# A hybrid decoder layer on one core: q and k stacks and most blocks of normalised x transposed on TensorE and copied out of PSUM by ScalarE, in place of DMA transposes

## Chip, cores and metric

The kernel runs on one core of one Trainium2 chip. The metric is the device time of one execution in microseconds (us), from the first to the last instruction and the little that lies around them. Lower is better.

## What is computed

One decoder layer on x of 2048 rows by 1024 columns, in float32: a normalisation, one wide input projection, three causal token mixers side by side, gates, and an output projection. Cut to what matters:

```python
h = rms_norm(x, norm_g)
proj = einsum('bsd,de->bse', h, w_in)          # fq fk fv fg ff px pg sq sk sv sg
fq, fk = rms_norm(heads(fq, 8), q_norm_g), rms_norm(heads(fk, 8), k_norm_g)
log_f = log_sigmoid(ff + b_f)
# A) forgetting attention, 8 heads of 64:
#    softmax(q.k/8 + c[t] - c[s], s <= t) @ v,  c = cumsum(log_f)
fox = forgetting_attention(fq, fk, fv, log_f) * silu(fg)
# B) causal means over 2, 4, 8, 16 rows, a small linear map per group
pool = multiscale_pool(px, w_pool, pool_scale) * silu(pg)
# C) stick-breaking attention, 4 heads of 64, z = q.k/8, s < t:
#    A[t,s] = sigmoid(z_ts) * prod_{s<j<t} (1 - sigmoid(z_tj))
sb = stick_breaking_attention(sq, sk, sv) * silu(sg)
out = x + concat([fox, pool, sb]) @ w_out
```

## The kernel before

Rows are worked on in 16 blocks of 128, last block first (block index i, row block j = 15 - i, so the keys that block i needs are those of blocks already done). Five phases follow each other and overlap: "a" (heads 0 to 3 of the forgetting attention), "b" (heads 4 to 7), "s" (stick-breaking, 4 heads), "p" (pooling, strewn between the blocks of "s") and "o" (output projection). Every number is kept as a pair of float16 values, a high part and the rest ("hi" and "lo"), so a product takes two or three matmuls.

For each block of phase "a" the rows of x are normalised, split into hi and lo (tile `ppx`, 128 x 2048 float16), and transposed into `xTx` (16 squares of 128) by one DMA transpose on SP's queue (`transpose_rows`, L375). The transposed block is parked in DRAM and read back in phases b, s and p. The projection (`project`, L319) then gives q and k in one PSUM tile and v and the gate in another. For q and k the function `stacks` (L455) makes a tile `st` (`sta`, `stb`, `sts` by phase) that holds k as hi and lo and q as hi and lo for four heads; one DMA transpose (L464) turns it into `qT`. Five steps of the projection later (`SCD`) `place` copies the k half into the key store `K` (L467) and swaps the two halves of q (L469, twice), all on VectorE. Scores (`scores`, L404) multiply `qT` with `K` into a PSUM tile with the tag `sp`. There are two buffers of that tag, each of two banks of PSUM, and each score tile holds one until VectorE (phases a and b, L736) or ScalarE (phase s, L875) has read it. The weights that come out are split into hi and lo (`split_t`: hi on ScalarE or VectorE L430 and L432, lo on GpSimd L433, tile `pp`), transposed by DMA (L435, tile `tt`) and multiplied with V (L446, L447, L903 to L905) three heads later. The tiles `pp` come from `PB` buffers.

A planner with its own estimate of every duration puts the instructions of each engine in order ahead of time; each engine then runs its list strictly in that order and waits at the head of it. Tables such as `LEADS` and `PAT` say how many projection steps are mixed in between the heads. All DMA transposes are issued from SP's queue. The clock of TensorE is granted by the chip, at 2.4 or 1.2 GHz.

Of the kernel before, what the change touches and what calls it, by code (L numbers as in the profile page):

```python
# [10 lines left out]
F16 = mybir.dt.float16  # L11
BF16 = mybir.dt.bfloat16
AF = mybir.ActivationFunctionType
ALU = mybir.AluOpType
# [4 lines left out]
P = 128  # L19
KT = 8  # L20
D = 1024
HD = 64
NH = 4
# [13 lines left out]
GR4 = 0  # L37
GR2 = 1
QSB = 2
SWE = 'vv'  # L40
KCE = 'v'
SCD = 5
M5 = 2
FE = 's'
OMS = 'g'
# [17 lines left out]
LEAD = 10  # L63
DEPTH = 3
TB = 4
PB = 5
FHIA = 'sv'
FHIB = 'ssv'
FLO = 'gg'
# [56 lines left out]
def hybrid(ctx: ExitStack, tc, xN, w_in, w_pT, w_out, ng, b_f, qg, kg, w_pool, p_scale, bands, out):  # L126
    nc = tc.nc
    v, s, g, t, sy = nc.vector, nc.scalar, nc.gpsimd, nc.tensor, nc.sync
# [4 lines left out]
    const = ctx.enter_context(tc.tile_pool(name="const", bufs=1))  # L133
# [3 lines left out]
    at = ctx.enter_context(tc.tile_pool(name="at", bufs=2))  # L137
    sm = ctx.enter_context(tc.tile_pool(name="sm", bufs=3))
    pj = ctx.enter_context(tc.tile_pool(name="pj", bufs=PJ, space=PSUM))
    ps = ctx.enter_context(tc.tile_pool(name="ps", bufs=2, space=PSUM))  # L140
# [5 lines left out]
    def pick(pattern, k):  # L146
        return {"v": v, "g": g, "s": s}[pattern[k % len(pattern)]]
# [31 lines left out]
    ident = const.tile([P, P], F32, name="ident")  # L179
# [4 lines left out]
    g.affine_select(tri, ones, [[-1, P]], ALU.is_ge, 0.0, base=0, channel_multiplier=1)  # L184
    id16 = const.tile([P, P], BF16, name="id16")
    g.tensor_copy(id16, ident)
    zero = at.tile([P, P], BF16, name="zero", tag="oa")
    g.memset(zero, 0.0)
    cmask = const.tile([P, P], BF16, name="cmask")
# [37 lines left out]
    class Weights:  # L227
# [12 lines left out]
        def measure(self, kt):  # L240
            for a, n in enumerate(self.widths):
                wr = self.raw(kt, a, "wm")
                junk = at.tile([P, n], BF16, name=f"jk{self.name}_{kt}_{a}", tag="pp", bufs=PB)
                acc = self.fa[:, a * KT + kt:a * KT + kt + 1]
# [53 lines left out]
        def weigh(self, kt, eng):  # L298
            held = self.held[:, kt]
            junk = at.tile([P, self.widths[0]], BF16, name=f"jh_{kt}", tag="L", bufs=LB) if eng is s else at.tile([P, self.widths[0]], BF16, name=f"jh_{kt}", tag="pp", bufs=PB)  # L300
            acc = self.fa[:, kt:kt + 1]
# [37 lines left out]
    def pairs16(hi, lo, src, scale, eng=v):  # L339

        s.activation(hi, src, AF.Copy, scale=scale)
        eng.scalar_tensor_tensor(lo, src, scale, hi, ALU.mult, ALU.subtract)  # L342
# [28 lines left out]
    def transpose_rows(src, scale, tag, park=None):  # L371
        pp = at.tile([P, 2 * D], F16, name=f"pp{tag}", tag="pp", bufs=PB)
        pairs16(pp[:, 0:D], pp[:, D:2 * D], src, scale[:, 0:1], pick(XLO, park or 0))
        x = xp.tile([P, 2, KT, P], F16, name=f"xT{tag}", tag="xT", bufs=XB)
        sy.dma_start_transpose(x.rearrange("p a k t -> p (a k) t"), pp)  # L375
        if park is not None:
            keep_x(park, x)
        return x

# [70 lines left out]
    def heads(ap):  # L450
        return ap.rearrange("p (h d) -> p h d", h=NH)
# [2 lines left out]

    def stacks(tag, j, qsrc, ksrc, sc, Kc):  # L455

        st = at.tile([P, 2, NH, P], F16, name=f"st{tag}", tag="qs", bufs=QSB)
        pairs16(st[:, 0, :, 0:HD], st[:, 0, :, HD:P], heads(ksrc), sc)
        pairs16(st[:, 1, :, 0:HD], st[:, 1, :, HD:P], heads(qsrc), sc)
        qT = at.tile([P, 2 * NH, P], F16, name=f"qT{tag}", tag="qT", bufs=QTB)  # L460
        if j % 4 == 3:
            Kc[j // 4] = big.tile([P, NH, 512], F16, name=f"K{tag}", tag="K", bufs=KB)
        o_ = (j % 4) * P
        sy.dma_start_transpose(qT, st.rearrange("p a h d -> p (a h d)"))  # L464

        def place():
            pick(KCE, 0).tensor_copy(Kc[j // 4][:, :, o_:o_ + P], qT[:, 0:NH])  # L467
            for k in range(2):
                pick(SWE, k).tensor_copy(qT[k * HD:k * HD + HD, 0:NH], qT[HD - k * HD:P - k * HD, NH:2 * NH])  # L469
            placed.add(tag)  # L470

        later(SCD, place)
        return qT
# [839 lines left out]
```

## Time and profile before

| | before |
|---|---|
| runs | 1418.04 us median of 3 (1412.04 to 1418.87) |
| the profiled execution | 1417.73 us |
| its span, first to last instruction | 1415.7 us |
| mean granted TensorE clock | 0.937 of 2.4 GHz |
| busy: TensorE, VectorE, ScalarE, GpSimd | 85%, 70%, 50%, 45% |
| mean busy share of the DMA engines, phases a and b | 97% |

The profiled execution lies 0.3 us under the median and 2.0 us over its own span. Phase a takes the span from about 46 to 462 us, b to 821 us, s (with p) to 1280 us, and the end of o the rest. Busy shares are means over these stages.

### The profile page before, as it was taken

What the parts mean: (1) busy time and instruction counts of PE and PEld (TensorE: products, weight loads), DVE (VectorE), ACT (ScalarE), POOL (GpSimd) and SP (SyncE); (2) the same over time, 40 slices, a digit from 0 to 9 for tenths busy, and PEclk for the clock granted to TensorE, in tenths of its full rate; (3) what the DMA queues carried; (4) which work ended last, traced back from release to release, by engine and by line L of the source; (5) the groups of instructions that cost most, each with busy time, mean ns of one, the idle gap of its engine ahead of it and who ended that gap; (6) DMA issues with size and microseconds to landing.
All of it is one profiled execution on the core that took longest, in us unless ns stands there. A gap on an engine that the chain in (4) does not pass through costs nothing.

```text
span 1415.7 us, 24981 instructions
## 1 busy us (share of the span) xinstructions
PE 1209.6 (85%) x9068; PEld 642.2 (45%) x9068; DVE 997.1 (70%) x2093; ACT 702.0 (50%) x1356; POOL 634.1 (45%) x615
## 2 busy tenths in 40 slices
PE   7788879787887889897987888978988997779998
PEld 3344445444444445454544544444544553444443
DVE  5777889889998567786888655556574669865731
ACT  6555546555554446664667644545455564432210
POOL 0133345445455234553656654555455464623300
PEclk9889899999998989999999999999999999989999
DMA  6689999998999999996999998687886888999853
GB/s 215 176 169 203 214 188 221 200 196 182 210 210 209 210 227 207 202 177 135 184 217 191 227 207 186 146 158 161 173 175 142 172 196 226 225 277 287 225 160 89
DMA packets 617068, 275.25 MB, mean 194 GB/s; under 512 B 552561, under 2 KB 590833, under 8 KB 616945
## 3 DMA queue, kind: packets, MB, share of 16 engines
q1 hardware_dynamic: 605600, 239.93, 80.4%
q10 hardware_dynamic: 10832, 33.67, 7.9%
q8 instruction: 71, 1.16, 0.4%
q14 instruction: 53, 0.43, 0.1%
q0 software_dynamic: 512, 0.07, 0.0%
HBM read 102.60 MB, written 34.67 MB: 97 GB/s over the span
## 4 chain that ended last, share of the span: by engine, by line
PE 18%; DVE 11%; issue 9%; DMA 8%; POOL 8%; ACT 5%; SPq 1%; POOLq 0%; ACTq 0%; DVEq 0%
PE pr L319 11%; DVE rrs L883 5%; POOL pps L433 5%; DMA qTs<-sts 2%; DMA qTb<-stb 2%; PE pqks L319 2%; DVE Lb L736 2%; DMA xTm<-ppm 1%; ACT pps L430 1%; ACT Lb L746 1%; POOL rrs L877 1%; PE sps L404 1%; DMA ttb<-ppb 1%; PE pp L319 1%; POOL ppb L433 1%
## 5 line engine op out<-in xcount | busy, mean ns | idle before, releaser
L433 POOL TENSOR_TENSOR ppb<-Lb,ppb 128x1024 f16<-128x1024 f32 (+7 forms) x96 | 151.6, 1593 | 150.3 <-ACT ppb L430 68.9
L433 POOL TENSOR_TENSOR ppa<-La,ppa 128x1024 f16<-128x1024 f32 (+7 forms) x96 | 152.7, 1604 | 141.9 <-DVE ppa L432 53.4
L433 POOL TENSOR_TENSOR pps<-rrs,pps 128x640 f16<-128x640 f32 (+7 forms) x96 | 171.3, 1790 | 75.2 <-ACT pps L430 74.8
L319 PE MATMUL pr<-wo,xTm 128*128 128x512 f16 x768 | 172.2, 386 | 8.1 <-DMA xTm<-ppm 5.3
L883 DVE TENSOR_TENSOR_SCAN rrs<-rrs 128x640 f32<-128x640 f32 (+7 forms) x64 | 109.5, 1714 | 68.3 <-POOL rrs L877 43.8
L430 ACT CAST pps<-rrs 128x640 f16<-128x640 f32 (+7 forms) x96 | 76.1, 796 | 142.0 <-DVE rrs L883 127.3
L746 ACT ACTIVATE Lb<-Lb,nmb 128x640 f32<-128x640 f32 (+7 forms) x96 | 85.6, 892 | 80.3 <-DVE nmb L740 75.4
L746 ACT ACTIVATE La<-La,nma 128x640 f32<-128x640 f32 (+7 forms) x96 | 85.5, 891 | 77.0 <-DVE nma L740 53.5
L319 PEld LDWEIGHTS <-xTm 128*128 128x128 f16 x768 | 75.8, 99 | 100.9 <-issue 8.8
L319 PEld LDWEIGHTS <-xTb 128*128 128x128 f16 x768 | 77.0, 103 | 92.6 <-issue 16.7
L404 PE MATMUL spa<-Ka,qTa 128*128 128x512 f16 (+3 forms) x320 | 83.7, 371 | 36.8 <-DVE mma L736 35.2
L319 PEld LDWEIGHTS <-xTs 128*128 128x128 f16 x768 | 74.4, 99 | 86.9 <-issue 3.3
L319 PEld LDWEIGHTS <-xTx 128*128 128x128 f16 x720 | 72.6, 105 | 89.3 <-issue 25.5
L319 PE MATMUL pqkb<-wb,xTb 128*128 128x512 f16 x384 | 101.7, 408 | 0.3 <-ACT wb L277 0.3
L404 PE MATMUL spb<-Kb,qTb 128*128 128x512 f16 (+3 forms) x320 | 79.7, 361 | 23.4 <-DVE mmb L736 20.7
L319 PE MATMUL pp<-auxp,xTp 128*128 128x512 f16 x384 | 96.9, 404 | 0.0
L319 PE MATMUL pqka<-wa,xTx 128*128 128x512 f16 x336 | 95.3, 434 | 1.3 <-DVE cr L562 1.3
L319 PE MATMUL pvgb<-wb,xTb 128*128 128x512 f16 x384 | 96.1, 390 | 0.0
L875 ACT ACTIVATE rrs<-sps,nc 128x640 f32<-128x640 f32 (+7 forms) x96 | 80.5, 863 | 30.3 <-PE sps L404 28.8
L319 PE MATMUL pqks<-ws,xTs 128*128 128x512 f16 x384 | 92.1, 385 | 0.7 <-DVE vo L342 0.4
L404 PE MATMUL sps<-Ks,qTs 128*128 128x512 f16 (+3 forms) x320 | 73.2, 361 | 21.2 <-DVE qTs L469 16.6
L319 PE MATMUL pvgs<-ws,xTs 128*128 128x512 f16 x384 | 90.9, 379 | 0.0
(307 smaller groups left out, 2804.4 us busy)
## 6 DMA issues: line engine op xcount, KB each, us to landing
xn<-in_xN_dram SPq DMA_DIRECT2D x16, 512.0 KB, 5.5
xTd<-xTx ACTq DMA_DIRECT2D x16, 512.0 KB, 4.3
xTb<-xTd ACTq DMA_DIRECT2D x16, 512.0 KB, 4.6
xTs<-xTd ACTq DMA_DIRECT2D x16, 512.0 KB, 4.3
xTp<-xTd ACTq DMA_DIRECT2D x16, 512.0 KB, 4.3
go<-gat SPq DMA_DIRECT2D x16, 512.0 KB, 7.6
mt<-mix SPq DMA_DIRECT2D x16, 512.0 KB, 5.6
xr<-in_xN_dram SPq DMA_DIRECT2D x16, 512.0 KB, 4.4
```

The costliest lines, as they stand in the source:

```text
L319: t.matmul(psum, x[:, xa, kt, :], wt[:, wa, c0:c0 + n], start=(kt == 0 and i == 0), stop=(kt == KT - 1 and i == 2))
L404: t.matmul(sp[:, b - c0 + off:e - c0 + off], qT[:, a * NH + h, :], Kc[b // 512][:, h, b % 512:b % 512 + e - b], start=(a == 0), stop=(a == ...
L430: s.copy(hi, p32)
L433: lo_eng.tensor_tensor(lo, p32, hi, ALU.subtract)
L736: v.tensor_tensor_reduce(lt, sp, negc[:, h, c0:c1_], c1[:, 0:1], 4 * NEG if a == 0 else mm[:, a - 1:a], ALU.add, ALU.max, mm[:, a:a + 1])
L746: s.activation(ls[a], ls[a], AF.Exp, bias=nm[:, 0:1], accum_out=la[:, a, h:h + 1])
L875: s.activation(gg, sp, AF.Sigmoid, scale=self.nc2[:, 0:1])
L877: g.affine_select(gg[:, 0:P], gg[:, 0:P], [[1, P]], ALU.is_gt, 1.0, base=0, channel_multiplier=-1)
L883: v.tensor_tensor_scan(gg, gg, gg, init, ALU.mult, ALU.bypass)
```

## The change

In `transpose_rows` the blocks that get parked are transposed by 16 TensorE transposes into a new PSUM tile `pt`, which takes one of the two `sp` buffers, and ScalarE copies it out in two pieces. In the program that is so for 14 of the 16 blocks of x; blocks 13 and 14, which the opening makes, and the 16 blocks of the output phase stay with the DMA. In `stacks` the tile `st` gets a third section: k as hi and lo, q's hi twice, q's lo twice. ScalarE writes hi of q over 512 instead of 256 columns, and VectorE makes lo of q in two passes instead of one. `place` makes 12 TensorE transposes into a `pt` tile, and two ScalarE copies bring out the keys and `qT`. The swap is no longer needed. `SCD` falls from 5 to 2 and `PB` from 5 to 4.

```diff
--- before.py
+++ after.py
@@ -37,9 +37,7 @@
 GR4 = 0
 GR2 = 1
 QSB = 2
-SWE = 'vv'
-KCE = 'v'
-SCD = 5
+SCD = 2
 M5 = 2
 FE = 's'
 OMS = 'g'
@@ -63,7 +61,7 @@
 LEAD = 10
 DEPTH = 3
 TB = 4
-PB = 5
+PB = 4
 FHIA = 'sv'
 FHIB = 'ssv'
 FLO = 'gg'
@@ -184,6 +182,8 @@
     g.affine_select(tri, ones, [[-1, P]], ALU.is_ge, 0.0, base=0, channel_multiplier=1)
     id16 = const.tile([P, P], BF16, name="id16")
     g.tensor_copy(id16, ident)
+    idh = const.tile([P, P], F16, name="idh")
+    g.tensor_copy(idh, ident)
     zero = at.tile([P, P], BF16, name="zero", tag="oa")
     g.memset(zero, 0.0)
     cmask = const.tile([P, P], BF16, name="cmask")
@@ -372,8 +372,14 @@
         pp = at.tile([P, 2 * D], F16, name=f"pp{tag}", tag="pp", bufs=PB)
         pairs16(pp[:, 0:D], pp[:, D:2 * D], src, scale[:, 0:1], pick(XLO, park or 0))
         x = xp.tile([P, 2, KT, P], F16, name=f"xT{tag}", tag="xT", bufs=XB)
-        sy.dma_start_transpose(x.rearrange("p a k t -> p (a k) t"), pp)
-        if park is not None:
+        if park is None:
+            sy.dma_start_transpose(x.rearrange("p a k t -> p (a k) t"), pp)
+        else:
+            pt = ps.tile([P, 2048], F16, name=f"pt{tag}", tag="sp")
+            for b in range(2 * KT):
+                t.transpose(pt[:, b * P:(b + 1) * P], pp[:, b * P:(b + 1) * P], idh)
+            for a in range(2):
+                s.copy(x[:, a], pt[:, a * D:(a + 1) * D].rearrange("p (k t) -> p k t", k=KT))
             keep_x(park, x)
         return x
 
@@ -454,19 +460,28 @@
 
     def stacks(tag, j, qsrc, ksrc, sc, Kc):
 
-        st = at.tile([P, 2, NH, P], F16, name=f"st{tag}", tag="qs", bufs=QSB)
+
+        st = at.tile([P, 3, NH, P], F16, name=f"st{tag}", tag="qs", bufs=QSB)
         pairs16(st[:, 0, :, 0:HD], st[:, 0, :, HD:P], heads(ksrc), sc)
-        pairs16(st[:, 1, :, 0:HD], st[:, 1, :, HD:P], heads(qsrc), sc)
+        hi, lo = (st[:, a].rearrange("p h (r d) -> p h r d", r=2) for a in (1, 2))
+        s.activation(hi, heads(qsrc).unsqueeze(2).broadcast_to([P, NH, 2, HD]), AF.Copy, scale=sc)
+        for r in range(2):
+            v.scalar_tensor_tensor(lo[:, :, r], heads(qsrc), sc, hi[:, :, r], ALU.mult, ALU.subtract)
         qT = at.tile([P, 2 * NH, P], F16, name=f"qT{tag}", tag="qT", bufs=QTB)
         if j % 4 == 3:
             Kc[j // 4] = big.tile([P, NH, 512], F16, name=f"K{tag}", tag="K", bufs=KB)
         o_ = (j % 4) * P
-        sy.dma_start_transpose(qT, st.rearrange("p a h d -> p (a h d)"))
 
         def place():
-            pick(KCE, 0).tensor_copy(Kc[j // 4][:, :, o_:o_ + P], qT[:, 0:NH])
-            for k in range(2):
-                pick(SWE, k).tensor_copy(qT[k * HD:k * HD + HD, 0:NH], qT[HD - k * HD:P - k * HD, NH:2 * NH])
+            pt = ps.tile([P, 2048], F16, name=f"pt{tag}", tag="sp")
+            for h in range(NH):
+                t.transpose(pt[:, 1024 + h * P:1024 + (h + 1) * P], st[:, 0, h, :], idh)
+            for a in range(2):
+                for h in range(NH):
+                    b = (a * NH + h) * P
+                    t.transpose(pt[:, b:b + P], st[:, 1 + a, h, :], idh)
+            s.copy(Kc[j // 4][:, :, o_:o_ + P], pt[:, 1024:1536].rearrange("p (h b) -> p h b", h=NH))
+            s.copy(qT, pt[:, 0:1024].rearrange("p (h b) -> p h b", h=2 * NH))
             placed.add(tag)
 
         later(SCD, place)
```

Counted over the program, 800 transposes come to TensorE, 124 copies to ScalarE and 48 passes to VectorE; 144 copies leave VectorE and 62 DMA transposes leave SP's queue. The planner then orders much anew. Three places, all at block 8 of the stick-breaking phase, show what the prediction speaks of. Names carry the block, the head and a buffer number.

TensorE before, from the last scores of block 7 (`sps_7_3`) through the projection of v and gate (`pvgs_8`) to the first scores of block 8 (`sps_8_0`):

```order
L404 MATMUL sps_7_3_0_11587<-Ks_0_9518,qTs_7_11141 128x512
...
L319 MATMUL pvgs_8_11549<-ws_6_9114,xTs7_11302 128x512
...
L319 MATMUL pvgs_8_11549<-ws_7_9119,xTs7_11302 128x512
L404 LDWEIGHTS qTs_8_11546
L404 MATMUL sps_8_0_0_11671<-Ks_8_11547,qTs_8_11546 128x128
...
L404 MATMUL sps_8_0_0_11671<-Ks_4_10419,qTs_8_11546 128x512
```

TensorE now, at the same place; `pts_8` is the new PSUM tile and `sts_8` the stack:

```order
L478 MATMUL pts_8_12290<-idh_157,sts_8_12275 128x128
...
L482 MATMUL pts_8_12290<-idh_157,sts_8_12275 128x128
...
L410 MATMUL sps_7_3_0_12336<-Ks_0_10157,qTs_7_11864 128x512
...
L319 MATMUL pvgs_8_12283<-ws_7_9745,xTs7_12036 128x512
L482 LDWEIGHTS sts_8_12275
...
L410 LDWEIGHTS qTs_8_12281
L410 MATMUL sps_8_0_0_12417<-Ks_8_12282,qTs_8_12281 128x128
```

Eight of the twelve transposes stand ahead of the scores of block 7, and the last four directly ahead of the first scores of block 8.

VectorE before, in the same stretch (the scans L883 are listed as SCALAR_TENSOR_TENSOR; `sts` is the lo part of the stack):

```order
L342 SCALAR_TENSOR_TENSOR sts_8_11541<-pqks_8_11438,sts_8_11541 128x4x64 x2
L883 SCALAR_TENSOR_TENSOR rrs_7_2_0_11525<-rrs_7_2_0_11525 128x1024
L910 SCALAR_TENSOR_TENSOR oms_6_11583<-os_6_11367,io_9126,oms_6_11583 128x256
L467 COPY Ks_8_11547<-qTs_8_11546 128x4x128
L469 COPY qTs_8_11546<-qTs_8_11546 64x512 x2
L883 SCALAR_TENSOR_TENSOR rrs_7_3_0_11592<-rrs_7_3_0_11592 128x1024
```

VectorE now:

```order
L342 SCALAR_TENSOR_TENSOR sts_8_12275<-pqks_8_12172,sts_8_12275 128x4x64
L898 SCALAR_TENSOR_TENSOR rrs_7_2_0_12259<-rrs_7_2_0_12259 128x1024
L469 SCALAR_TENSOR_TENSOR sts_8_12275<-pqks_8_12172,sts_8_12275 128x4x64 x2
L925 SCALAR_TENSOR_TENSOR oms_6_12332<-os_6_12101,io_9752,oms_6_12332 128x256
L898 SCALAR_TENSOR_TENSOR rrs_7_3_0_12341<-rrs_7_3_0_12341 128x1024
```

The three copies that wait for the DMA are gone from between the scans, and the two passes for q's lo stand behind one scan more.

ScalarE now, in the same stretch (`pps` is the hi part of the split, L890 the sigmoid of the scores); before, there were no COPY rows here:

```order
L467 ACTIVATE sts_8_12275<-pqks_8_12172 128x512
L436 CAST pps_7_2_0_12266<-rrs_7_2_0_12259 128x1024
L890 ACTIVATE rrs_7_3_0_12341<-sps_7_3_0_12336,nc2_9750 128x1024
L391 DMA xTp13_12040<-xTd13_126 128x2048
L483 COPY Ks_8_12282<-pts_8_12290 128x4x128
L484 COPY qTs_8_12281<-pts_8_12290 128x1024
L436 CAST pps_7_3_0_12348<-rrs_7_3_0_12341 128x1024
```

The two copies that the first scores of block 8 need stand on ScalarE behind a cast that waits for a scan and a sigmoid that waits for the scores of block 7.

## Rows read from the trace of the kernel before

**Rows 1.** The page: span, busy time and share of two engines.

```profile
span 1415.7 us, 24981 instructions
PE 1209.6 (85%) x9068; PEld 642.2 (45%) x9068; DVE 997.1 (70%) x2093; ACT 702.0 (50%) x1356; POOL 634.1 (45%) x615
```

**Rows 2.** Four stretches: length, busy us (instructions) by engine, granted clock, DMA share, GB/s.

```profile
46.00:462.00 416.00, 342.84 (x2594) 185.83 (x2593) 350.29 (x943) 222.88 (x511) 188.81 (x150) 0.91 0.97 201
462.00:821.00 359.00, 309.03 (x2313) 169.25 (x2312) 260.22 (x610) 207.14 (x435) 180.60 (x154) 0.95 0.97 197
821.00:1280.00 459.00, 393.10 (x3418) 211.08 (x3415) 292.58 (x347) 222.96 (x333) 236.53 (x286) 0.94 0.85 189
1280.00:1416.00 136.00, 129.32 (x608) 58.19 (x603) 64.77 (x98) 18.68 (x17) 25.32 (x9) 0.99 0.64 187
```

**Rows 3.** DMA issues: engine, number, median us from issue to landing.

```profile
xTx<-ppx SPq DMA_TRANSPOSE x16, 4.5
...
qTs<-sts SPq DMA_TRANSPOSE x16, 3.7
```

**Rows 4.** Waits of VectorE: us in total, times, longest.

```profile
DVE Ks L467 <- DMA qTs<-sts: 35.5, 12, 5.4
...
DVE Kb L467 <- DMA qTb<-stb: 23.5, 12, 5.9
...
DVE Ka L467 <- DMA qTa<-sta: 13.9, 8, 3.0
```

**Rows 5.** Waits of TensorE: us in total, times, longest.

```profile
PE spa L404 <- DVE mma L736: 35.2, 20, 4.9
PE spb L404 <- DVE mmb L736: 20.7, 13, 4.1
PE ob L446 <- DMA ttb<-ppb: 20.6, 16, 3.9
...
PE sps L404 <- DVE qTs L469: 16.6, 5, 7.1
PE pf L328 <- DMA xTx<-ppx: 11.0, 7, 2.8
PE oa L446 <- DMA tta<-ppa: 10.7, 6, 3.2
PE os L903 <- DMA tts<-pps: 8.6, 8, 3.1
```

**Rows 6.** The chain that ended last, shares of the span by engine and line.

```profile
PE 18%; DVE 11%; issue 9%; DMA 8%; POOL 8%; ACT 5%; SPq 1%; POOLq 0%; ACTq 0%; DVEq 0%
PE pr L319 11%; DVE rrs L883 5%; POOL pps L433 5%; DMA qTs<-sts 2%; DMA qTb<-stb 2%; PE pqks L319 2%; DVE Lb L736 2%; DMA xTm<-ppm 1%; ACT pps L430 1%; ACT Lb L746 1%; POOL rrs L877 1%; PE sps L404 1%; DMA ttb<-ppb 1%; PE pp L319 1%; POOL ppb L433 1%
```

**Rows 7.** VectorE in order of time: start, length, idle before it, releaser.

```profile
934.96 0.29 DVE L467 COPY Ks<-qTs 128x512 f16<-128x512 f16 x1 [4.46 <-DMA qTs<-sts]
```

**Rows 8.** TensorE in order of time, same stretch.

```profile
935.93 2.10 PE L404 MATMUL sps<-Ks,qTs 128*128 128x128 f16 x6 [7.12 <-DVE qTs L469]
```

**Rows 9.** The window after that wait, columns as in group 2, with TensorE loads second.

```profile
936.00:943.00 7.00, 7.00 (x58) 3.81 (x59) 6.05 (x5) 4.72 (x8) 4.05 (x4) 0.81 0.36 72
```

**Rows 10.** TensorE in order of time: nine pairs of V matmuls, then scores.

```profile
601.58 0.22 PE L446 MATMUL ob<-Vb,ttb 128*128 128x128 f16 x1
...
602.34 0.38 PE L404 MATMUL spb<-Kb,qTb 128*128 128x256 f16 x2
```

**Rows 11.** ScalarE groups of one shape: busy us, mean ns, idle before.

```profile
L430 ACT CAST pps<-rrs 128x1024 f16<-128x1024 f32 x28 | 29.2, 1044 | 55.0 <-DVE rrs L883 43.7 <-DMA tts<-pps 6.3 <-DVE mx L1038 5.0
...
L430 ACT CAST pps<-rrs 128x512 f16<-128x512 f32 x20 | 12.4, 618 | 15.8 <-DVE rrs L883 14.4 <-DMA tts<-pps 1.4
```

**Rows 12.** All work of L469, then of L467, on VectorE: us (instructions).

```profile
0.00:1416.00 1416.00, 51.07 (x96) 0.94 0.89 194
...
0.00:1416.00 1416.00, 26.30 (x48) 0.94 0.89 194
```

**Rows 13.** All lo passes into `stb` on VectorE: us (instructions).

```profile
0.00:1416.00 1416.00, 22.85 (x32) 0.94 0.89 194
```

## The prediction, made before the change was run

> **What bounds the kernel now.** I read the page first. TensorE is busy 1209.6 of 1415.7 us, the longest of all engines, so it stands idle for 206 us [rows 1]. The windows by stage show that this holds throughout: TensorE is busy 82% in phase a, 86% in b and 86% in s, at a granted clock of 0.91, 0.95 and 0.94. The DMA engines are nearly full beside it, 0.97 of their time in a and b and 0.85 in s, and VectorE is busy 84% of phase a [rows 2]. So two resources are close to full in a and b, and the change moves work from the fuller one, the DMA, to the other. The list of waits then says what the 206 us are made of. TensorE waits 55.9 us for VectorE to empty a score buffer (35.2 in a, 20.7 in b), 39.9 us for transposed weights to land (20.6, 10.7 and 8.6), 16.6 us for the swapped q of phase s, and 11.0 us for a transposed x [rows 5]. Last I read the chain that ended last. TensorE is 18% of the span there. The landings of transposed stacks of s and b are 2% each, some 57 us together [rows 6]. VectorE's own list shows why they lie there: its copies into the key store stand at the head of its queue for 35.5 + 23.5 + 13.9 = 72.9 us until a stack has landed [rows 4].
>
> One place shows the mechanism. At block 8 of phase s VectorE stands idle for 4.46 us, until the stack has landed at 934.96 us [rows 7], copies and swaps, and TensorE, which has no other work ahead of the scores, has by then waited 7.12 us [rows 8].
>
> **The change, part by part.** Time here is TensorE's busy time, its idle time, and 2 us around the span, so each part is priced by what it does to one of these. I start from the profiled execution, 1417.7 us, which lies 0.3 us under the median of the runs shown; that difference is left out.
>
> Transposes on TensorE. There are 48 x 12 + 14 x 16 = 800. Each streams 128 columns and has a load of 128 columns of its own, like the first matmul of a pair with V. Nine such pairs, each of 128 and 64 columns, take 602.34 - 601.58 = 0.76 us from start to start, 84 ns for 192 columns, so 56 ns for 128 [rows 10]. That makes 45 us at 2.4 GHz, and 48 us at the mean granted clock of 0.937. How much of it moves the end is bounded by two rows. TensorE's 18% stand in a chain that reaches back over about 60% of the span (the sum of its shares), which is 30% [rows 6]: then 14 us. Its busy share is 85% [rows 1]: then 41 us. Neither is nearer, since the list is in order but the waits behind a transpose can shrink by what is put ahead of them. I take the middle, **+28 us**.
>
> The same row speaks on a rule of the Trainium skill, page "TensorE: Matmul & The Clock Gate", section "Part 4: PE-mode transpose". It says that a 128 x 128 transpose was measured at about 275 ns within a kernel. By that figure 800 would cost an estimated 220 us, and the sum below would be some 1610 us; that speaks strongly against the change. The rows of this case give the same kind of duration for one matmul, 0.22 us, while the next starts 56 ns later, so I take the spacing for the price, and the sum does not use the page's figure.
>
> Copies on ScalarE. Nothing in the trace copies float16 out of PSUM there; the nearest rows are the casts of 1024 columns at 1.04 us and 512 columns at 0.62 us [rows 11]. So 48 x (1.04 + 0.62) + 28 x 1.04 = 109 us, and the wider q passes add at most 48 x 0.2 = 10 us. The engine goes from 702 to about 820 us, 58% of the span, and is at most 58% busy in any stage of the trace before, so most of it lies beside other work. On the chain ScalarE is 5 of 60 parts, 8% [rows 6], which gives **+10 us**. The lower bound is 0. The upper is half of it, 60 us, if the copies were queued behind scans as often as ScalarE is busy. Queued behind them are sigmoids and exponentials, so the scores' buffers and GpSimd's split would come later.
>
> VectorE. The copies and swaps that go were 51.1 + 26.3 = 77.4 us [rows 12], and the 72.9 us of standing at the head go too. The 48 extra passes come to 48 x 0.71 = 34 us by those into `stb`, 22.85 us for 32 [rows 13]. Net some 116 us of 1070 us, 11%, leave a queue that TensorE waits 55.9 us for. By that share **-6 us**; bounds 0 and, if every such wait came from the stacks, -56.
>
> The path of q. Before, a stack took a landing of 3.7 us [rows 3] and 77.4/48 = 1.6 us of copies, 5.3 us. Now, once the stack is there, four or twelve transposes (0.2 to 0.7 us) and two copies (1.7 us) come to 1.9 to 2.4 us, so some two thirds of the wait goes. The smaller price for that wait is TensorE's own, 16.6 us [rows 5], two thirds of which is 11. The larger is the chain's 57 us [rows 6], two thirds of which is 38. I take the middle, **-25 us**: not all of VectorE's late scans delay a matmul. In most blocks the planner puts much matmul work between the transposes and the first scores; at the place shown it puts none, so there ScalarE's copies are the next thing to be late.
>
> The path of x. 11.0 us of waits [rows 5] came with a landing of 4.5 us [rows 3]. Now 16 transposes and two copies are 0.9 + 2.1 = 3.0 us. A third goes, **-4 us**; bounds 0 and -11.
>
> DMA load. By the shapes, phase a transposed 35.7 MB of weights, 8.4 of x and 4.2 of stacks; 7.3 and 4.2 MB leave, 24%. In b and s 4.2 of 39.9 MB leave, 10.5%. If waits for weights fall in proportion, 0.24 x 10.7 + 0.105 x (20.6 + 8.6) is **-6 us**. They could fall by all 39.9 if the 0.97 were the whole cause, or not at all: each weight tile waits three heads in the pipeline anyway, and `PB` falls from 5 to 4, which takes a buffer from the same tiles.
>
> The score buffers. The two `sp` buffers now also serve 62 transposes, 46 of them in a and b beside 192 score tiles. A score tile waits 55.9/192 = 0.29 us on average there [rows 5]; at that price 46 more users cost **+13 us**. Bounds: 0, where the planner finds a free buffer, and 46 x 1.66 = 76 us, if the tile behind each one always waits for both copies. Most tiles did not wait at all (33 of 192 did), so the low value is nearer.
>
> SP's 62 issues and the planner's other moves I cost at nothing, since SP's queue waits for data, not the other way, and a transfer that starts sooner is covered by the three heads between split and use; without that cover a start delayed by one issue would cost about a landing, 4 us, each time. The sum: 28 + 10 - 6 - 25 - 4 - 6 + 13 = +10, so 1417.7 + 10 = **1428 us**.
>
> **The rivals.**
>
> The chain is right (chance 0.30). VectorE's stand for a landing was what delayed everything, and the nearly full DMA lets go too: the q path gives 38 us, x 4, VectorE 6, and the weights half of their 39.9, 20; the transposes cost the chain's 14 and the copies 10. That is 1417.7 - 44 = 1374 us. For it: the chain's 57 us, and the 7 us at block 8. Against: TensorE's direct waits for q are only 16.6 us. It decides from where the gains exceed about 50 us.
>
> Nothing is left of it (0.18): gains and costs cancel within 7 us of 1418. This is the case where transposes fill the waits and ScalarE delays as much as the landing did.
>
> The ring (0.11). Each `pt` tile holds one of two score buffers until two queued copies are through, and scores of a and b stall. Half of the upper price, 38 us, in place of 13 gives 1453 us. For it: the 33 waits of the longest kind in TensorE's list. Against: TensorE waits there for only 5% of those stages. It decides if the mean wait per transpose passes 0.8 us.
>
> The clock (0.07). After TensorE's long wait at block 8 the granted clock over the next seven microseconds is 0.81, part of it at 1.2 GHz, though TensorE is then busy without a gap [rows 9]. If the transposes were to the chip as idle time, each of the 62 groups would be a chance for that. A window like this one loses 0.19 x 7 = 1.3 us, so one for every group adds 62 x 1.3 = 81 us, and one for every third 27 us: 1455 us. Against it stands that none of these groups lasts a microsecond, while the wait shown lasted seven. The page named above says in the same section that transposes do not count as busy for the clock gate; no row of this trace can show it.
>
> **How the numbers follow.** The forecast, 1428 us with its own range of 1422 to 1445, is the likeliest with 0.34. A measurement of this kernel cannot tell less than about 0.5%, 7 us, from no change. Of the forecast's 0.34, 0.06 falls within 7 us of 1418; of the case of no change 0.03 lies just beyond on each side. So slower is 0.28 + 0.11 + 0.07 + 0.03 = 0.49, same 0.18 - 0.06 + 0.06 = 0.18, faster 0.30 + 0.03 = 0.33. The range of 8 in 10 goes from 1370, the chain's case with a little more, to 1460, beyond the ring and the clock at their middle prices. The upper bounds of single costs are left out at both ends.
>
> **What would show it.** Right: TensorE's busy time up by some 48 us, its waits for landed x and swapped q nearly gone, new waits of TensorE on ScalarE's copies or for a score buffer, DMA share in a near 0.75 to 0.85, VectorE's head waits of 72.9 us gone. Wrong: TensorE's idle time falling by more than 50 us, above all in waits for VectorE and for weights, would mean that the DMA and VectorE's queue bound these stages; busy time up by far more than 48 us would mean the clock.

## The result

| | before | after |
|---|---|---|
| runs | 1418.45 us median of 4 (1412.04 to 1420.55) | 1475.7 us median of 4 (1471.76 to 1484.31) |
| ratio to before | | 1.042, 95% interval 1.0363 to 1.0476 |
| span of the profiled execution | 1415.7 us | 1470.0 us |
| mean granted TensorE clock | 0.937 | 0.938 |

Slower was right, but the loss is 57 us where 10 were forecast, and the time lies 16 us above the range of 8 in 10 (1370 to 1460). First the page of the kernel after: span, then busy time, share and instructions by engine; [rows 1] answer to it.

```profile
span 1470.0 us, 26481 instructions
PE 1246.1 (85%) x9868; PEld 690.2 (47%) x9868; DVE 952.1 (65%) x1997; ACT 808.2 (55%) x1479; POOL 625.3 (43%) x616
```

The span grew by 54.3 us: TensorE's busy time by 36.5, its idle time by 17.8. The windows of the same four stages (columns as in [rows 2], with the loads of weights second) say where.

```profile
54.00:507.00 453.00, 357.63 (x2983) 208.97 (x2983) 329.83 (x874) 274.15 (x559) 185.52 (x148) 0.90 0.69 153
507.00:884.00 377.00, 321.19 (x2530) 182.68 (x2531) 244.45 (x587) 239.28 (x474) 177.46 (x153) 0.94 0.83 177
884.00:1336.00 452.00, 397.18 (x3563) 218.96 (x3562) 276.30 (x315) 238.99 (x358) 235.78 (x290) 0.96 0.81 182
1336.00:1470.00 134.00, 127.58 (x584) 57.19 (x582) 65.83 (x104) 20.78 (x19) 22.91 (x9) 0.99 0.67 195
```

Against [rows 2], the opening ahead of a is 8 us longer, a 37 and b 18, while s is 7 us shorter and the end 2 us shorter. In a the DMA engines fell from 0.97 to 0.69 of their time, VectorE and GpSimd did less, and still the stage grew: no engine is full there. So the waits have to be read, TensorE's first (us in total, times, longest; [rows 5] has those of before).

```profile
PE ob L452 <- DMA ttb<-ppb: 31.6, 14, 11.5
PE oa L452 <- DMA tta<-ppa: 31.5, 18, 5.6
PE ptx L380 <- ACT ppx L341: 23.7, 5, 11.7
PE spa L410 <- DVE mma L751: 15.5, 13, 4.4
PE pts L478 <- DVE sts L342: 12.2, 5, 5.2
PE spb L410 <- DVE mmb L751: 9.5, 11, 2.2
...
PE ptb L478 <- DVE mma L751: 6.3, 2, 4.8
...
PE os L918 <- DMA tts<-pps: 5.3, 5, 2.7
```

The waits named in the prediction did fall: for a score buffer from 55.9 to 25.0 us, and x and q no longer appear as landed tiles. But TensorE now waits for something it never waited for, the split rows that it is to transpose (`ppx`, `sts`): all waits ahead of a `pt` tile add up to 64.7 us, of which 44.0 are for split rows and 12.2 for a score buffer to come free. And it waits 68.4 us for transposed weights (31.6, 31.5 and 5.3), where it was 39.9. ScalarE, which never waited for TensorE's transposes before, has its own new list.

```profile
ACT Kb L483 <- PE ptb L482: 34.6, 11, 12.1
ACT xTx L382 <- PE ptx L380: 22.3, 9, 4.5
ACT Ka L483 <- PE pta L482: 11.1, 6, 5.6
ACT Ks L483 <- PE pts L482: 9.8, 8, 3.2
```

Together 77.8 us: the copy stands at the head of ScalarE's list, the exponentials and casts of the scores behind it. One place in a shows the two lists at work, in order of time (start, length, engine, what, and in brackets the idle time before it and what ended it).

```profile
303.08 1.58 DVE L221 TENSOR_TENSOR q_qka<-fa 128x8 f32<-128x8 f32 x1 [0.17 <-ACT fa L219]
304.70 3.49 DVE L222 TENSOR_TENSOR q_qka<-q_qka,ssa 128x8 f32<-128x8 f32 x1
...
308.96 0.47 ACT L505 ACTIVATE gta<-pvga,iwa 128x256 f32<-128x256 f32 x1 [5.08 <-DVE Va L342]
...
310.36 1.04 ACT L352 ACTIVATE xj<-xn 128x1024 bf16<-128x1024 f32 x1
...
313.39 1.15 ACT L341 ACTIVATE ppx<-xn,r 128x1024 f16<-128x1024 f32 x1 [0.94 <-DVE r L360]
...
314.60 1.03 PE L380 MATMUL ptx<-idh,ppx 128*128 128x128 f16 x8 [11.74 <-ACT ppx L341]
...
318.12 1.01 ACT L382 COPY xTx<-ptx 128x1024 f16<-128x1024 f16 x1 [3.58 <-PE ptx L380]
```

TensorE is done with its projection at 302.9 us, and next in its list are the transposes of x. Their rows are not split yet: VectorE is held up by 5 us in two small steps, ScalarE stands for it, then squares x (310.36), and only at 313.39 splits it. TensorE stands for 11.74 us with scores behind the transposes. Before, DMA transposes waited in SP's queue, beside TensorE: ahead of those of the stacks (L464) that queue stood 75.7 us in all. Then ScalarE stands 3.58 us, since even the first of the two copies starts only when the transposes of the second half are done (318.08). And over the 3.4 us after its wait the granted clock of TensorE is 0.50, the lower of its two levels (length, busy us by engine, granted clock, DMA share, GB/s):

```profile
314.60:318.00 3.40, 3.40 (x21) 2.43 (x22) 1.99 (x2) 0.00 (x0) 0.00 (x0) 0.50 0.56 111
```

The longest of ScalarE's waits is the mirror image, in b:

```profile
521.89 0.29 PE L452 MATMUL ob<-Vb,ttb 128*128 128x128 f16 x1 [11.49 <-DMA ttb<-ppb]
...
528.56 0.39 PE L478 MATMUL ptb<-idh,stb 128*128 128x128 f16 x4
...
529.43 0.58 ACT L483 COPY Kb<-ptb 128x512 f16<-128x512 f16 x1 [12.12 <-PE ptb L482]
```

TensorE waits for weights; behind that wait stand a projection, at a granted clock of 0.60 from 521.9 to 529 us, then a stack's transposes, and behind these ScalarE's copy. ScalarE's next exponentials need scores that TensorE makes only after that (529.23), so the splits come late to GpSimd, SP and the DMA, and with them the next weights. The waits of SP's queue fit that: it stands for GpSimd's lo pass 105.8 us in a, where the same wait in the kernel before was 50.2 us, while a transpose of a's weights lands faster (4.2 us, before 4.7). After, then before:

```profile
SPq L441 <- POOL ppa L439: 105.8, 50, 8.7
```

```profile
SPq L435 <- POOL ppa L433: 50.2, 31, 5.5
```

### The profile page after: what moved, and what is told of

Same layout as the page of the kernel before. It is cut to its first block, busy times and chain, and to the rows that moved or that the text cites. A ratio compares the mean times of both kernels' runs of the same rounds, so it can differ in the third digit from the quotient of the medians.

```text
span 1470.0 us, 26481 instructions
## 1 busy us (share of the span) xinstructions
PE 1246.1 (85%) x9868; PEld 690.2 (47%) x9868; DVE 952.1 (65%) x1997; ACT 808.2 (55%) x1479; POOL 625.3 (43%) x616
## 4 chain that ended last, share of the span: by engine, by line
PE 40%; DVE 16%; DMA 15%; ACT 11%; issue 10%; POOL 7%; SPq 1%; ACTq 0%; POOLq 0%; DVEq 0%
PE pr L319 11%; PE pqkb L319 4%; POOL pps L439 4%; DMA ttb<-ppb 4%; DVE rrs L898 4%; DMA tta<-ppa 3%; PE pqka L319 3%; PE pvga L319 3%; DMA tts<-pps 3%; PE pqks L319 2%; PE spb L410 2%; PE spa L410 2%; PE pvgb L319 2%; DVE Lb L751 2%; DVE La L751 2%
## 5 line engine op out<-in xcount | busy, mean ns | idle before, releaser
L439 POOL TENSOR_TENSOR pps<-rrs,pps 128x640 f16<-128x640 f32 (+7 forms) x96 | 176.5, 1841 | 87.2 <-ACT pps L436 86.7
L319 PE MATMUL pr<-wo,xTm 128*128 128x512 f16 x768 | 171.6, 385 | 10.2 <-DMA xTm<-ppm 8.5
L319 PEld LDWEIGHTS <-xTb 128*128 128x128 f16 x768 | 73.4, 100 | 84.0 <-issue 9.6
L319 PEld LDWEIGHTS <-xTx 128*128 128x128 f16 x720 | 68.7, 101 | 75.4 <-issue 10.8
L751 DVE CUSTOM_DVE_ANT_0 Lb<-spb,negcb,c 128x640 f32<-128x640 f32 (+7 forms) x64 | 60.4, 947 | 57.0 <-PE spb L410 32.1
L319 PE MATMUL pvgb<-wb,xTb 128*128 128x512 f16 x384 | 95.8, 392 | 0.0
L319 PE MATMUL pqkb<-wb,xTb 128*128 128x512 f16 x384 | 93.4, 386 | 2.7 <-ACT wb L277 2.7
L319 PE MATMUL pp<-auxp,xTp 128*128 128x512 f16 x384 | 90.2, 383 | 0.9 <-DVE vo L342 0.9
L452 PE MATMUL oa<-Va,tta 128*128 128x128 f16 x544 | 63.0, 228 | 32.8 <-DMA tta<-ppa 31.5
L890 ACT ACTIVATE rrs<-sps,nc 128x640 f32<-128x640 f32 (+7 forms) x96 | 81.0, 865 | 14.7 <-PE sps L410 8.3
```

Of the source, the lines that this page charges most:

```text
L319: t.matmul(psum, x[:, xa, kt, :], wt[:, wa, c0:c0 + n], start=(kt == 0 and i == 0), stop=(kt == KT - 1 and i == 2))
L439: lo_eng.tensor_tensor(lo, p32, hi, ALU.subtract)
L452: t.matmul(o[:, 0:P], tt[:, b, :], vt, start=first, stop=False)
L751: v.tensor_tensor_reduce(lt, sp, negc[:, h, c0:c1_], c1[:, 0:1], 4 * NEG if a == 0 else mm[:, a - 1:a], ALU.add, ALU.max, mm[:, a:a + 1])
L890: s.activation(gg, sp, AF.Sigmoid, scale=self.nc2[:, 0:1])
```

## The experiments

Three theories. **The lists**: the transposes and copies are written into the program, and so into TensorE's and ScalarE's lists, before their rows are ready, and hold up what stands behind them. **The work**: 45 us more of TensorE and 104 us of copies more on ScalarE. **The fifth buffer**: `PB` fell from 5 to 4. Every kernel was timed against the kernel before on its own chip, where that one had medians of 1414.7 to 1418.5 us. In the table a, b and s run from the first score matmul of a phase to that of the next (s: to its last score matmul), and the last two columns are summed from the lists of waits: TensorE's ahead of any `pt` tile, and ScalarE's for one. These columns come from one profiled execution each; for "x alone, 10 steps late" it lies 10 us above the median, for the last row 11.

| kernel | median us | ratio to before, 95% | a | b | s | TensorE at `pt` | ScalarE for `pt` |
|---|---|---|---|---|---|---|---|
| before | | | 386.5 | 355.2 | 440.1 | 0 | 0 |
| after | 1475.7 | 1.042 (1.0363, 1.0476) | 425.8 | 373.6 | 432.5 | 64.7 | 77.8 |
| before, 4 split buffers | 1425.2 | 1.0077 (1.0033, 1.0121) | 390.4 | 352.2 | 447.3 | 0 | 0 |
| before, 800 idle transposes | 1437.1 | 1.0145 (1.0108, 1.0182) | 389.5 | 363.6 | 444.4 | 0 | 0 |
| before, placing 12 steps late | 1415.4 | 1.0012 (0.9984, 1.004) | 382.2 | 359.9 | 441.4 | 0 | 0 |
| stacks alone | 1485.8 | 1.0484 (1.0456, 1.0513) | 430.1 | 376.6 | 437.2 | 57.7 | 54.4 |
| stacks alone, 5 steps | 1447.4 | 1.0208 (1.0152, 1.0264) | 416.8 | 356.1 | 435.5 | 48.7 | 24.1 |
| x alone | 1458.8 | 1.03 (1.0257, 1.0343) | 413.0 | 361.3 | 444.7 | 10.2 | 24.1 |
| x alone, 10 steps late | 1425.0 | 1.0081 (1.0048, 1.0113) | 382.9 | 358.8 | 451.9 | 14.3 | 7.3 |
| the same, 5 split buffers | 1406.5 | 0.9891 (0.9829, 0.9954) | 374.1 | 350.3 | 445.8 | 13.6 | 4.6 |
| after, 5 steps | 1453.2 | 1.0236 (1.017, 1.0302) | 423.4 | 360.5 | 431.4 | 56.0 | 39.8 |
| after, copies on VectorE | 1481.3 | 1.0465 (1.0402, 1.0528) | 427.0 | 380.8 | 435.5 | 79.9 | 0 |
| after, 5 split buffers | 1482.2 | 1.0464 (1.0431, 1.0497) | 448.8 | 361.6 | 432.1 | 57.5 | 48.7 |
| after, x 10, stacks 5 steps | 1443.2 | 1.0177 (1.0129, 1.0225) | 413.3 | 360.1 | 431.8 | 48.4 | 22.9 |
| the same, 5 split buffers | 1446.0 | 1.0211 (1.0174, 1.0247) | 416.3 | 362.6 | 430.4 | 51.7 | 28.4 |
| after, x 10, stacks 9 steps | 1410.3 | 0.9949 (0.9918, 0.998) | 382.6 | 353.6 | 435.6 | 27.7 | 12.3 |
| the same, 5 split buffers | 1397.4 | 0.9847 (0.98, 0.9894) | 382.4 | 340.8 | 439.5 | 26.8 | 20.3 |
| after, 12 and 12 steps, 5 buffers | 1386.2 | 0.9791 (0.9751, 0.983) | 367.9 | 349.3 | 430.2 | 20.5 | 9.8 |
| after, 14 and 16 steps, 5 buffers | 1408.2 | 0.9965 (0.9941, 0.9988) | 378.0 | 353.9 | 437.9 | 14.0 | 20.2 |
| x 10, only s's stacks, 5 buffers | 1392.9 | 0.983 (0.9772, 0.9888) | 372.4 | 360.6 | 432.7 | 24.7 | 15.4 |

**The parts by themselves.** Four split buffers in the kernel before:

```diff
-PB = 5
+PB = 4
```

> The kernel before with 4 instead of 5 of the buffers for split rows (pp), and nothing else. Three theories of the 57 us: 'the lists' (TensorE's transposes of x wait at the head of its list for ScalarE and VectorE, and ScalarE's copies wait behind TensorE), 'the fifth buffer' (one pp buffer fewer makes the split of the softmax rows and so the DMA transposes later, seen in the waits for tta and ttb, 31 us before and 63 us after), and 'the work' (800 transposes are 45 us of a TensorE that was busy 85% of the span). The fifth buffer expects 1440 to 1465 us here, with the waits for tta and ttb near 60 us. The lists and the work expect 1414 to 1425 us.

Slower by 0.8%, while TensorE's waits for weights fell, from 39.9 to 19.4 us. The fifth buffer by itself is a small part of the 4.2%, and the sum of one kind of wait is no price: it can fall while the kernel gets slower. Next, the stacks alone (x goes through the DMA again), and x alone (`stacks` and `SCD` as before):

```diff
-        if park is None:
-            sy.dma_start_transpose(x.rearrange("p a k t -> p (a k) t"), pp)
-        else:
...
+        sy.dma_start_transpose(x.rearrange("p a k t -> p (a k) t"), pp)
+        if park is not None:
             keep_x(park, x)
```

> The kernel after, but the rows of x go through the DMA transpose again; only the stacks of q and k are transposed on TensorE (576 of the 800 transposes, 96 of the 124 copies; 4 pp buffers). The lists expect most of the loss gone: 1415 to 1435 us, the stage of a near 420 us instead of 453. The work expects 576/800 of 57 us, 1459 us. The fifth buffer expects the same as the kernel before with 4 buffers, and the stacks at nothing.

> The kernel after, but the stacks of q and k go through the DMA transpose, VectorE's copies and the delay of 5 steps again; only the rows of x are transposed on TensorE (224 of the 800 transposes, 28 of the 124 copies; 4 pp buffers). The lists expect most of the loss here: 1445 to 1465 us, with the stage of a at 440 us or more and b and s as before. The work expects 224/800 of 57 us, 1434 us. The fifth buffer expects the same as the kernel before with 4 buffers.

The lists as I first had them, with x as the cause, fell: the stacks alone cost more than the whole change, x alone seven tenths of it, and the two don't add up. For the stacks alone all the numbers that I gave were too low. But both lose in a, and both have the new waits. The list of the stacks alone, TensorE's and then ScalarE's:

```profile
PE pts L473 <- DVE sts L342: 16.8, 5, 6.5
PE pta L473 <- DVE sta L342: 11.2, 3, 6.0
...
ACT Ka L478 <- PE pta L477: 23.3, 9, 5.4
ACT Kb L478 <- PE ptb L477: 21.5, 8, 8.3
```

Then TensorE's work without waits, copies or buffers, put into `scores` of the kernel before (n is 4 or 5 in a, 2 in b and s, 800 in all):

```diff
         sp = ps.tile([P, 1024], F32, name=f"sp{tag}", tag="sp")
+        to = sp.bitcast(BF16)
+        for b in range(n):
+            t.transpose(to[:, b * P:(b + 1) * P], id16, id16)
```

> The kernel before with 800 more transposes of a constant on TensorE, written into each score buffer just before its score matmuls overwrite it (4 or 5 per buffer in a, 2 in b and s): TensorE's work of the change without any of its waits, copies or buffers. They are 45 us of TensorE at 56 ns. The work expects most of it in the time: 1450 to 1475 us. The lists expect TensorE's waits to take up much of it: 1430 to 1445 us.

It cost 21 us (15 to 26), of which 3 in a. So TensorE's work cannot be what makes a 39 us longer. Its page:

```profile
span 1430.9 us, 26581 instructions
PE 1234.5 (86%) x9868; PEld 683.0 (48%) x9868; DVE 978.0 (68%) x2093; ACT 703.9 (49%) x1356; POOL 636.4 (44%) x615
```

**Later in the lists.** The same transposes and copies, written later into the program. For a stack it is `SCD`, for x a delay of its own (the first of the 14 blocks is not put off):

```diff
-SCD = 2
+SCD = 5
```

```diff
-            pt = ps.tile([P, 2048], F16, name=f"pt{tag}", tag="sp")
...
-            keep_x(park, x)
+            def turn():
+                pt = ps.tile([P, 2048], F16, name=f"pt{tag}", tag="sp")
...
+                keep_x(park, x)
+
+            later(10 if park < NT - 3 else 0, turn)
```

> Only the stacks on TensorE, x by the DMA transpose, and the placing of a stack put off by 5 steps as in the kernel before instead of 2. With 2 steps this kernel was 70 us longer than the one before, and TensorE stood 42 us at the head of its list for a stack's split (pta, ptb, pts). 'The lists' (a transpose put into an engine's list before its rows are there holds everything behind it): most of the 60 us beyond the fifth buffer's 9 go: 1425 to 1455 us, and the waits for the stacks' split fall below 15 us. 'The work and the copies' (what TensorE and ScalarE have more to do): 1470 to 1490 us, as with 2 steps.

> Only the rows of x on TensorE, the stacks as before, and now x's 16 transposes and 2 copies come 10 steps later in the program than x's split, still ahead of their use. Without the delay it was 43 us longer than the kernel before. 'The lists' as the split of x is waited for at the head of TensorE's list (ptx 9.5 us there, 23.7 in the kernel after): 1425 to 1445 us, ptx waits under 3 us. If the cause lies elsewhere (buffers, the planner's order): 1450 to 1465 us.

> The kernel after with the placing of a stack put off by 5 steps instead of 2, nothing else. 'The lists': a part of its 57 us goes, those that hang on the stacks; 1435 to 1460 us, the waits of TensorE for a stack's split (12.2 pts, 6.3 ptb, 3.7 pta) near nothing. 'The work and the copies': 1470 to 1480 us.

All three gained: 38 us for the stacks alone, 34 us for x alone, and 22 us for the kernel after, where only the stacks were put off. x alone lost all that lay above the kernel with 4 buffers (1425.0 and 1425.2 us), and a is at 382.9 us. TensorE's wait for `ppx`, which I had expected under 3 us, did not fall there (10.2 and 10.6 us); it was ScalarE's wait for `ptx` that did, and TensorE's for weights, from 51.7 to 30.9 us. The other two are alike in this: the last column of the table falls by about half, the one before it by 9 us. ScalarE's wait before the delay and after it:

```profile
ACT xTx L384 <- PE ptx L382: 24.1, 9, 6.4
```

```profile
ACT xTx L386 <- PE ptx L384: 7.3, 6, 2.0
```

With the stacks I had expected TensorE's waits for their split below 15 us; they were still 28.1 us, 17.6 of them in a in 5 times, so 5 steps may have been too few. Is it that ScalarE is the wrong engine?

```diff
-                s.copy(x[:, a], pt[:, a * D:(a + 1) * D].rearrange("p (k t) -> p k t", k=KT))
+                v.tensor_copy(x[:, a], pt[:, a * D:(a + 1) * D].rearrange("p (k t) -> p k t", k=KT))
```

(and so for `K` and `qT`)

> The kernel after with its 124 copies out of PSUM on VectorE instead of ScalarE, nothing else. ScalarE had 109 us more of work by them, and its list mixes them with the exponentials and casts of the score path. 'Copies on ScalarE' as the cause: 1430 to 1455 us. 'The lists' (TensorE's in-order list and its waits for the split rows): no better than 1470 us, since VectorE stands in the same chain.

No gain: ScalarE no longer waits for `pt`, but VectorE now does (19.6 us), and TensorE's waits ahead of `pt` rise to 79.9 us. With this order the other engine for the copies changed nothing that the intervals can tell (1.042 and 1.0465).

**Both delays, and the buffers.** 5 split buffers beside the larger `st` fit only with 2 buffers of `qT` instead of 3 (`QTB`), so the kernels after with 5 have both; x alone has room for 3.

> The kernel after with both delays: a stack is placed 5 steps later instead of 2, and x's transposes and copies come 10 steps after x's split. Nothing is taken away: all 800 transposes, all 124 copies, 4 pp buffers. By 'the lists' the two delays add up, as each does on its own (21 us from the stacks' in the kernel after, 34 from x's where only x is on TensorE): 1415 to 1435 us. By 'the work and the copies', which the delays leave as they are, at least the 21 us that TensorE's work alone cost: 1440 us or more.

> The kernel after with x 10 steps and the stacks 5 steps later, 5 pp and 2 qT buffers. It differs from the one of 1443 us by the buffers and from the one of 1397 us by the stacks' 5 instead of 9 steps. If the steps did it: 1430 to 1440 us. If the buffers did it: 1395 to 1410 us.

> The kernel after with x's transposes 10 steps and the stacks' 9 steps later, still with 4 pp buffers and 3 of qT. With 5 steps for the stacks it took 1443 us, with 9 steps, 5 pp and 2 qT buffers 1397 us. If the steps did it: 1400 to 1415 us. If the buffers did it: 1435 to 1445 us. If each needs the other: between.

> All on TensorE with x delayed by 10 steps and stacks by 9, and 5 pp buffers, for which qT gets 2 buffers instead of 3. 'The lists' and 'the fifth buffer' together: 1405 to 1425 us. If two qT buffers are too few, or a later placing makes the scores wait: over 1430 us.

> The kernel after with 5 pp buffers again, for which qT gets 2 buffers instead of 3; the delays as in the kernel after (2 steps for a stack, none for x). 'The lists' as the first cause: the early transposes still stand in front of everything, 1455 to 1470 us, 9 us or a little more won back. 'The fifth buffer' as the first cause (with 4 buffers nothing can run ahead, so any late link is felt): 1415 to 1435 us.

The two delays of 10 and 5 steps did not add up as I expected: 1443 us lies in the range that I had given to "the work and the copies", 1440 us or more. The corners of the table settle it against them. With 2 steps for the stacks (and none for x) or with 5 the fifth buffer, paid for with the third `qT`, gives nothing: the median is 7 and 3 us longer with it, and the first, 1482 us, lies above all that I had given for it. What the two `qT` buffers cost by themselves was not tried. The step from 5 to 9 gives 33 us with 4 buffers and 49 with 5; only then does the buffer count, 13 us, and that kernel is faster than I gave it (1397 us for 1405 to 1425). From the kernel after to the one with 10 and 9 steps nothing is taken away, every transpose, every copy, 4 buffers and two score buffers stay, and 65 us go, so that it lies 0.5% below the kernel before. A delay in the program lets the planner order all lists anew, so no single pair of instructions is isolated by it; but what was changed is the order alone. From the kernel after over 5 steps, 10 and 5, to 10 and 9, all with 4 buffers, the two sums of waits together go 142.5, 95.8, 71.3, 40.0 us and the median 1475.7, 1453.2, 1443.2, 1410.3 us. As a price the sums don't serve across kernels: x alone has 34.3 us of them and is 3.0% slower than the kernel before. Nor do the delays separate TensorE's list from ScalarE's, as each puts off transposes and copies together. With 10 and 9 steps ScalarE's waits for `pt` are these:

```profile
ACT Kb L487 <- PE ptb L486: 6.0, 4, 2.6
ACT xTx L384 <- PE ptx L382: 3.8, 6, 1.3
ACT Ka L487 <- PE pta L486: 2.5, 3, 1.8
```

With x alone the buffer counts too:

> Only x on TensorE, delayed by 10 steps, stacks as before, and 5 pp buffers again. It lay 10 us above the kernel before with 4 buffers, and the kernel before with 4 buffers lay 9 us above the one with 5. 'The fifth buffer' is then all that is left: 1410 to 1420 us. If x on TensorE costs its own work, 1420 to 1428 us.

19 us, more than the 9 that I put down to it, and already faster than before.

**Where it ends.** Longer delays, and the stacks on TensorE in phase s alone (a, b by DMA):

> The kernel after with x's transposes and the stacks' both 12 steps later, 5 pp and 2 qT buffers. If the delay is still too short at 10 and 9 steps (TensorE waits 17 us for tta and 5 us for x's copies there): 1385 to 1395 us. If the scores now wait for their late q and k: over 1400 us.

> The kernel after with x's transposes 14 and the stacks' 16 steps later, 5 pp and 2 qT buffers. With 12 and 12 steps it took 1386 us. If the delay has done its work by 12 steps: 1383 to 1392 us. If the projections then wait for x's copies (used at step 16) and the scores for q and k: 1392 to 1410 us.

> x on TensorE delayed by 10 steps, the stacks on TensorE in phase s alone (by 5 steps), in a and b by the DMA transpose; 5 pp and 2 qT buffers. Phase s was 5 to 9 us shorter with its stacks on TensorE in every run so far, a and b were longer. 1400 to 1412 us if that adds up, and then faster than the kernel before; 1415 to 1430 us if the two qT buffers take it back.

12 and 12 steps make the fastest kernel, 2.1% below the one before, by a few steps more and by the fifth buffer; the one with s's stacks alone lies close by, lower than either number I gave for it. The page of the fastest:

```profile
span 1381.3 us, 26513 instructions
PE 1224.1 (89%) x9868; PEld 680.0 (49%) x9868; DVE 939.9 (68%) x1997; ACT 800.5 (58%) x1479; POOL 637.6 (46%) x616
```

Its window from the first score of a to the first of b (columns as above):

```profile
59.20:427.10 367.90, 321.44 (x2780) 189.39 (x2780) 308.16 (x837) 252.44 (x527) 177.43 (x137) 0.95 0.83 177
```

And that of the kernel after:

```profile
59.70:485.50 425.80, 336.14 (x2778) 195.80 (x2778) 315.68 (x830) 260.01 (x528) 173.94 (x138) 0.90 0.68 152
```

Almost the same instructions of TensorE (2780 and 2778) take 15 us less of it and 58 us less of time. The stalls cost twice: the time itself, and a granted clock of 0.90 instead of 0.95 over the stage. Over the whole span, from the kernel after to this one, TensorE's idle time falls by 66.7 us and its busy time by 22.0, the clock being 0.938 and 0.959. With 14 and 16 steps 22 us are lost again, in all three phases. TensorE's waits at `pt` fall further there, ScalarE's double, and the waits for weights go from 32.6 to 43.4 us; which of these is first was not tried. The first score came 4 to 10 us later in every kernel with the new transposes (at 58.8 to 64.2 us, in the kernel before at 54.4); no delay took that back, and its cause stays open. The last question is whether the delay alone does it:

> The kernel before, all by DMA, with its placing of a stack (VectorE's copies of k and q) put off by 12 steps instead of 5, nothing else. If the gain of the delayed kernels is a matter of the delay alone, which the kernel before could have had too: 1380 to 1400 us. If the delay only takes away waits that TensorE's transposes bring in: 1405 to 1420 us, less VectorE's waits for a landed q and k (73 us of head waits in the kernel before).

It does not: with DMA transposes, 12 steps change nothing that can be measured, and VectorE still stands at the head for a landed stack (39.5, 26.3 and 15.9, together 81.7 us, where [rows 4] have 72.9).

## Why the prediction was wrong

**The paths of q and x (-25 and -4).** This is the step that failed. It said "once the stack is there, four or twelve transposes and two copies", and so priced a transpose from the moment its rows are ready. It asked neither what TensorE does until then nor what stands behind it. The DMA transpose waited in SP's queue, at the side; the new ones wait in TensorE's list and their copies in ScalarE's, 64.7 and 77.8 us in the two lists, each passing its lateness to the other. The fall of `SCD` from 5 to 2 got no price. Putting the same instructions later is worth 65 us, from 1.042 to 0.995 of the time before. The terms' own content was right: where TensorE waited 11.0 us for landed x and 16.6 for swapped q, it now waits 0.8 and 4.2 us for ScalarE's copies of them, and VectorE's 72.9 are gone. That slower came true does not speak for the sum: all the work that its positive terms price is still there in the fastest kernel, which is 2.1% faster than the one before.

**Transposes (+28).** About right: 21 us measured alone, within 14 to 41. TensorE's busy time rose by 25 us there and not by 48, as the clock was 0.953 there, not 0.937. In the kernel after it rose by 36.5. The page of the Trainium skill that the prediction weighed, "TensorE: Matmul & The Clock Gate", section "Part 4: PE-mode transpose", would have made that an estimated 220 us (and the sum 1620 us, not the 1610 given); the spacing in the rows was the better price.

**Copies (+10).** 103.6 us of ScalarE measured (1.02 and 0.58 us each), 109 estimated. What they cost as work is not separated; the fastest kernel has them all, and moving them to VectorE changed nothing that can be measured. The bound of 60 us spoke of what stands ahead of the copies in ScalarE's list, but meant scans and not TensorE's late transposes, and the range left it out.

**VectorE (-6), DMA (-6).** Score buffer waits fell by 31 us, and weights wait 28.5 us more, not 6 less: the landing is shorter, the start later. "The planner's other moves" and SP's issues at nothing was the same mistake as the paths: the cover of three heads did not hold where ScalarE's and GpSimd's splits came late. `PB` had its cost only as a bound; it is 9 us by the medians (5 to 17 by the interval) in the kernel before.

**Score buffers (+13), and the rivals.** Transposes waited 12.2 us for a score buffer and scores of a and b 25.0, together less than the 55.9 before, and two buffers also serve the fastest kernel. So waits for the ring did not make the loss; a third buffer was not tried. (The 5% that the prediction held against this rival should be 7%, 55.9 of 775 us.) Nor did the clock make it: its mean stayed at 0.938, and it was higher with 800 more transposes. The same section of that page says that transposes do not count as busy for the clock gate; no run here shows them pulling it down. The rival that gains, 1374 us, is not far from what the change gives with the lists in another order, 1386 us; which of its terms gave that was not measured.

Of what I named as the signs of right, VectorE's head waits and those for landed x went, and new waits on ScalarE's copies and for a score buffer came and were small. TensorE's busy time rose by 36.5 us and not 48, and the DMA share in a fell to 0.69, below the 0.75 to 0.85 that I gave. The waits that decided, TensorE's for rows not yet split and ScalarE's for the transposes behind them, stood in none of the cases.

## What to carry to other kernels

Work that is moved from a side queue into the list of a busy engine takes its wait along: price the time from its place in the list to its data being ready, and all that stands behind it, before its duration. If such a change loses while no engine is full, move the new instructions later in the program before giving it up; here 10 and 9 steps, with nothing else changed, were the difference between 4.2% slower and 0.5% faster, and 12 and 12 with one more split buffer made it 2.1% faster. Change one delay at a time and then the buffers: here the buffer gave nothing until the order was right.

## What was not expected of the hardware

TensorE's added work came partly for free: with 800 transposes ahead of the scores the mean granted clock was 0.953 instead of 0.937 in the two traces (0.949 to 0.953 in all four runs, 0.937 to 0.943 in the kernel before on the same chip), which on 1210 us is worth 1210 x (1 - 0.937/0.953) = 20 us, and busy time rose by 25 us where 800 x 56 ns are 45. And two VectorE steps on 128 x 8 elements (median of L222 there: 168 ns) took 1.58 and 3.49 us at 303 us, each ending when a lo pass of GpSimd ended:

```profile
301.17 3.47 POOL L439 TENSOR_TENSOR ppa<-La,ppa 128x512 f16<-128x512 f32 x2
...
305.16 2.99 POOL L439 TENSOR_TENSOR ppa<-La,ppa 128x896 f16<-128x896 f32 x2
```

The Trainium skill says, on the page "SBUF — State Buffer", section "Who interferes with whom", that VectorE shares one pair of ports with GpSimd under an exclusive lock, and that a VectorE instruction with two inputs in SBUF contends with a GpSimd instruction that reads SBUF. These rows agree with it, as each of the two VectorE steps ends within 0.04 us of a lo pass; whether GpSimd held them up was not tried.
